# Hybrid block on one core: shift columns partly from transposed weight rows on VectorE, the second V projection and the low-rank projection from rows without shift

## The chip, the cores and the metric

The kernel is one launch on one NeuronCore of a Trainium2 chip. The metric is device time in microseconds; several runs of a kernel are given as their median. A profile is one execution recorded by the hardware profiler.

## The reference, cut to what matters

The program is one layer: a norm with modulation, an input projection, a gated linear attention beside a short convolution, an output projection, a second norm and a feed-forward block. The change touches only the front of it:

```python
mx = silu(c) @ w_mod + b_mod            # c: (2048,), w_mod: (2048, 12288)
mc = silu(c_ctx) @ w_mod + b_mod
sh1, sc1, ... = split(mx, 6)            # shift: columns 0..2047; scale: 2048..4095
hx = rmsnorm(x, norm1_g) * (1 + sc1) + sh1        # x: (512, 2048)
hc = rmsnorm(ctx, norm1_g) * (1 + sc1c) + sh1c    # ctx: (256, 2048)
q, k, v, g, lf, lb, cb, cc, cx = split(hx @ w_in) # for ctx: k, v, lf, lb are needed
```

lf and lb, 16 columns each, are the low-rank projection from which the forget gates come. A projection of `hx` is linear in the shift. So (row without shift) @ w, scaled by the row's norm factor, plus one row sh1 @ w that is the same for all tokens, gives the same values. The kernel uses this, before and after, in different places.

## The kernel before, in words

All operands are fp32. A large product is done as three products of two-part numbers: `split` (L105) writes a high part with ScalarE (L106) and the low rest with VectorE (L107), `split_scaled` and `split_shifted` (L109, L114) do so with a factor or a shift on the way, and `mm3` (L96) issues three matmuls: low times high, high times low, high times high. Every matmul of the front is recorded at L94. Small products are plain fp32 matmuls, which the profile shows as two records each.

Tokens lie along the free dimension: `hx[i]` and `hc[i]`, 16 chunks of 128 channels, each as a high and a low tile, 512 columns for x and 256 for the context. The front has these stages, each a loop over the 16 chunks:

- **K pass** (L254 to L265). `scaled_chunk` multiplies raw rows by the scale alone and accumulates their squares; TensorE makes K from them. After it the norm factors `r6` come, and `rbx`, `rbc`, the same factors along the columns (L284 to L294).
- **First V pass** (L345 to L360). Six accumulators (four token tiles of x, two of the context), 18 matmuls a chunk: V columns 0 to 511, from rows that have neither norm factor nor shift. Beside it, after every fourth chunk, `mod_cols(wsh, ...)` computes the shift of four chunks by small TensorE products: 16 loads of 256 KB from `wsh`, 16 plain matmuls of 512 columns with the 32-column `silu(c)` tile as weights (tile `pm`), a copy `tm`, four small matmuls into `pc` that turn it to columns, four additions of the bias into `shs`. Four chunks later `shift_chunk(i)` rewrites the chunk: GpSimd adds the two parts (L307), VectorE multiplies by the norm factor (L308) and adds the shift (L311), and the sum is split again; for x and for the context. `lf_part` multiplies the low-rank weights with finished x chunks (tile `pl`).
- **Second V pass** (L463 to L478). V columns 512 to 1023 from the rewritten rows, with the last four `shift_chunk` calls. `shares(i)`, 16 calls, loads K and first-V weights again in raw form and makes the products `shs` times weights (tile `pb`): after eight calls the sum is spread to all rows (`pbc`, `pbx`) and added to K or V. The same calls make the context's low-rank products from the old context rows, added up by GpSimd (`hs`, L424).
- Then `weave` (L564) runs the context's states, q, g, the convolution and the attention, and `mod_some` (L380) makes the other four modulation vectors from transposed rows `wm2` with VectorE: a 128x1024 tile times `cbc` (silu(c) on all partitions) summed along the row by one `tensor_tensor_reduce` (L405). Of these loads some are issued by GpSimd, behind a one-element copy that makes them wait (L392).

Order is set by the tile framework: it plans each engine's queue from program order and its own estimate of costs, and may pull an instruction ahead of waiting ones; after that each engine runs its queue strictly in order. So a matmul of `pm` can stand between matmuls of the V pass. SyncE's queue (SP) issues the weight loads in the same way. Raw weight tiles `raw` (128x1024, 512 KB) go through four buffers; `whi` and `wlo`, the split weights, have three each; general tiles `big` have 24. PSUM has three banks of tag "a" and five of tag "g"; a V pass takes three of each.

Of the kernel before, what the change touches and what calls it, by code (L numbers as in the profile page):

```python
# [43 lines left out]

B_ID, B_ONE = range(2)
# [8 lines left out]
def tile_hybrid_block(  # L54
    ctx: ExitStack,
    tc: tile.TileContext,
    xT, cT, xr, ccol, crow, fgrow, cid, cst, sm, cols, gates,
    wsc, wsh, wm2, wk, wv, wl, wq, wg, wc, wo, wu, wd,
# [242 lines left out]
    hraw = {}  # L301

    def shift_chunk(i):

        for n, h, rb, q in ((SEQ, hx[i], rbx, 0), (CTX, hc[i], rbc, 1)):
            t = big() if q == 0 else hcpool.tile([P, n], F32, tag="sq1", name="ht", bufs=2)
            nc.gpsimd.tensor_tensor(t, h[0].bitcast(F32), h[1].bitcast(F32), op=ALU.add)  # L307
            nc.vector.tensor_tensor(t, t, rb, op=ALU.mult)  # L308
            sh = shs[:, i, q : q + 1]
            if q == 0:  # L310
                nc.vector.tensor_scalar(t, t, sh, None, op0=ALU.add)  # L311
                split(h[0], h[1], t)
                hraw[i] = t
            else:
                split_shifted(h[0], h[1], t, sh)
# [6 lines left out]
    def lf_part(pl, g):  # L322

        for j in range(4):
            mm(pl[32 * j : 32 * j + 32, :], wl3[:, 4 * g + j, :], hraw[4 * g + j], g == 0, g == 3)

    def lf_finish(pl, a, n):
# [7 lines left out]
        nc.vector.tensor_copy(lfT[64:96, a : a + n], ps[64:96, :n])  # L335

# [6 lines left out]
    for d in range(2):  # L343
        nc.vector.memset(lfT[64 * d + 32 : 64 * d + 33, :], 1.0)
    accv = banks6()  # L345
    pl = bank("pl")
    for i in range(KD):
# [4 lines left out]
        if i % 4 == 3:  # L352
            pcs = mod_cols(wsh, i - 3, 4)
            for c in range(4):
                nc.vector.tensor_scalar(shs[:, i - 3 + c, 0:2], pcs[:, 2 * c : 2 * c + 2], col(C_BMOD + i - 3 + c),
                                        None, op0=ALU.add)
        if i >= 4:
            shift_chunk(i - 4)
        if i in (8, 12):
            lf_part(pl, i // 4 - 2)  # L360
# [13 lines left out]
    nc.sync.dma_start(cbc, crow.partition_broadcast(P))  # L374
    nc.scalar.activation(cbc, cbc, AF.Silu)
# [40 lines left out]
    def shares(i):  # L416

        if i == 0:
            sh_t["pl"] = bank("pl")
        pl = sh_t["pl"]  # L420
        if i % 2 == 0:
            t = sh_t[i % 4] = hcpool.tile([P, 2, CTX], F32, tag="sq0", name="hs", bufs=2)
            for c in range(2):
                nc.gpsimd.tensor_tensor(t[:, c, :], hc[i + c][0].bitcast(F32), hc[i + c][1].bitcast(F32), op=ALU.add)  # L424
        if i % 4 == 3:
            for c in range(4):
                mm(pl[32 * c : 32 * c + 32, :CTX], wl3[:, i - 3 + c, :], sh_t[c // 2 * 2][:, c % 2, :], i == 3, i == 15)
# [3 lines left out]
        w = load_raw((wk if i < 8 else wv[0])[i % 8]).rearrange("p (k n) -> p k n", k=2)  # L431
# [4 lines left out]
        if i % 8 == 7:  # L436
            t = hcpool.tile([P, SEQ], F32, tag="lfs", name="bs", bufs=1)
            nc.scalar.copy(t, pb)
            pbc = bank("pbc")
            mm(pbc, cstt[:, B_SELC, :], t, True, True)  # L440
            if i < 8:
                for tt in range(NCT):
# [21 lines left out]
    for i in range(KD):  # L464
# [4 lines left out]
        if i < 4:  # L469
            shift_chunk(KD - 4 + i)  # L470
# [876 lines left out]
```

## Time and profile before

| what | us |
|---|---|
| median of 3 runs (2282.64 to 2289.99) | 2288.15 |
| the profiled execution, whole | 2291.32 |
| its span, first to last instruction | 2289.5 |
| first matmul of the first V pass, after the K pass | about 108.2 |
| last small products of the shift (`pc`) | 216.3 |
| first matmul of the next stage (q), after the second V pass | 300.0 |

The profiled execution is 1.8 us longer than its span, and 3.2 us longer than the median. A row of groups reads: line, engine, operation, tile written <- tiles read, shapes, count, then busy time in us and mean ns of one, then idle time before it. A row of the timeline reads: start, duration, engine, line, operation, count merged, and in brackets the idle time before it with what ended it. Matmuls overlap in their pipeline, so the start of the next one is a better measure of what one costs than its duration.

### The profile page before, as it was taken

To read this page: it belongs to the slowest core of one execution; us is meant where nothing else is said; L and a number is where in the kernel's file an instruction comes from. 1 tells how busy PE (TensorE), PEld (TensorE's weight loads), DVE (VectorE), ACT (ScalarE), POOL (GpSimd) and SP (SyncE) were. 2 spreads that over 40 slices of the span, in tenths; PEclk is the share of its full clock that TensorE was granted. 3 is DMA by queue.
4 is the path that set the end of the run, shared out by engine and by line. 5 is a ranking of instruction groups with operands and counts; after the bars stand their busy time and mean duration, and the time that the engine had idled before them with its cause. 6 is when DMAs were issued, how large, how long until landed. Compare 5 with 4: busy or idle time off the path is not lost.

```text
span 2289.5 us, 28001 instructions
## 1 busy us (share of the span) xinstructions
PE 2241.7 (98%) x10258; PEld 1791.7 (78%) x10258; DVE 1658.7 (72%) x2069; ACT 1002.6 (44%) x1354; POOL 251.0 (11%) x396
## 2 busy tenths in 40 slices
PE   8999999999999999999999999999999999999997
PEld 4765666787888887777888888888888878888886
DVE  3566165665768656899788879877987877787885
ACT  3433155333233433665555455445544544433343
POOL 2433100222332000100000000000000000000000
PEclk9999999999999999999999999999999999999999
DMA  9683465566767354624543464345435676756752
GB/s 329 216 279 129 153 221 189 202 220 202 250 228 258 116 198 157 208 69 141 189 156 120 147 210 148 118 159 172 158 131 183 246 291 212 244 193 206 253 174 93
DMA packets 163410, 433.16 MB, mean 189 GB/s; under 512 B 18022, under 2 KB 38790, under 8 KB 163144
## 3 DMA queue, kind: packets, MB, share of 16 engines
q1 hardware_dynamic: 128984, 331.20, 43.3%
q0 software_dynamic: 22416, 78.66, 9.7%
q10 hardware_dynamic: 11872, 21.52, 2.5%
q8 instruction: 81, 1.33, 0.2%
q14 instruction: 57, 0.47, 0.1%
HBM read 380.95 MB, written 50.35 MB: 188 GB/s over the span
## 4 chain that ended last, share of the span: by engine, by line
issue 56%; POOL 2%; PE 1%; DVE 1%; ACT 0%; DMA 0%; POOLq 0%; DVEq 0%; ACTq 0%
POOL opd L1066 2%; PE acc L94 1%; DVE wlo L107 0%; DVE ch L849 0%; DMA out<-g 0%; DVE u L1019 0%; POOL xnd L1022 0%; ACT whi L106 0%; POOL hbig L958 0%; DVE hbig L1020 0%; DVE u L869 0%; POOLq L1066 0%; ACT y L1214 0%; ACT acc L1205 0%; DVE g L1202 0%
## 5 line engine op out<-in xcount | busy, mean ns | idle before, releaser
L106 ACT CAST whi<-ch 128x1024 fp32r<-128x1024 f32 x335 | 352.5, 1053 | 415.4 <-PE acc L94 344.9
L107 DVE TENSOR_TENSOR wlo<-ch,whi 128x1024 fp32r<-128x1024 f32 x335 | 408.2, 1223 | 126.9 <-ACT whi L106 126.0
L106 ACT CAST whi<-raw 128x1024 fp32r<-128x1024 f32 x258 | 270.7, 1050 | 453.6 <-PE acc L94 282.0
L107 DVE TENSOR_TENSOR wlo<-raw,whi 128x1024 fp32r<-128x1024 f32 x258 | 316.6, 1227 | 198.3 <-ACT whi L106 197.7
L94 PE MATMUL acc<-hhl,whi 128*128 128x512 f32 x640 | 200.0, 393 | 0.0
L94 PEld LDWEIGHTS acc<-hhl,whi 128*128 128x128 f32 x640 | 120.8, 189 | 27.6 <-issue 2.5
L1066 POOL DMA_DIRECT2D opd<-ol x80 | 43.3, 541 | 885.8 <-DVE ol L107 885.7
L94 PE MATMUL acc<-hhi,wlo 128*128 128x512 f32 x320 | 134.1, 421 | 5.4 <-DVE wlo L107 4.6
L405 DVE CUSTOM_DVE_ANT_0 wm<-wm,cbc 128x1024 f32<-128x1024 f32 x66 | 80.6, 1224 | 80.9 <-DMA wm<-wm 80.2
L94 PE MATMUL acc<-wlo,a0h 128*128 128x512 f32 x324 | 128.8, 397 | 4.0 <-DVE wlo L107 4.0
L94 PE MATMUL acc<-whi,a6l 128*128 128x512 f32 (+1 forms) x330 | 127.9, 389 | 2.4 <-ACT acc L1205 2.1
L94 PE MATMUL acc<-wlo,a6h 128*128 128x512 f32 (+1 forms) x330 | 128.1, 388 | 1.3 <-DVE wlo L107 1.3
L94 PE MATMUL acc<-whi,a6h 128*128 128x512 f32 (+1 forms) x330 | 127.8, 387 | 0.0
L94 PE MATMUL acc<-whi,a0h 128*128 128x512 f32 x324 | 127.5, 393 | 0.0
L94 PE MATMUL acc<-hlo,whi 128*128 128x512 f32 x320 | 126.9, 397 | 0.2 <-DVE hlo L112 0.2
L94 PE MATMUL acc<-hhl,wlo 128*128 128x512 f32 x320 | 127.0, 397 | 0.0
L94 PE MATMUL acc<-whi,a0l 128*128 128x512 f32 x324 | 126.9, 393 | 0.0
L94 PE MATMUL acc<-whi,a5h 128*128 128x512 f32 x324 | 126.3, 390 | 0.0
L94 PE MATMUL acc<-hhi,whi 128*128 128x512 f32 x320 | 126.2, 394 | 0.0
L94 PE MATMUL acc<-whi,a5l 128*128 128x512 f32 x324 | 126.2, 389 | 0.0
L94 PE MATMUL acc<-wlo,a5h 128*128 128x512 f32 x324 | 126.1, 389 | 0.0
L405 DVE CUSTOM_DVE_ANT_0 raw<-raw,cbc 128x1024 f32<-128x1024 f32 x62 | 75.4, 1223 | 51.4 <-DMA raw<-wm 51.1
(334 smaller groups left out, 4991.8 us busy)
## 6 DMA issues: line engine op xcount, KB each, us to landing
raw<-wu SPq DMA_DIRECT2D x92, 512.0 KB, 4.4
ch<-wu SPq DMA_DIRECT2D x88, 512.0 KB, 3.8
wm<-wm POOLq DMA_DIRECT2D x66, 512.0 KB, 5.3
raw<-wd SPq DMA_DIRECT2D x50, 512.0 KB, 5.3
raw<-wc SPq DMA_DIRECT2D x48, 512.0 KB, 4.7
opd<-oh ACTq DMA_DIRECT2D x80, 256.0 KB, 3.2
opd<-ol POOLq DMA_DIRECT2D x80, 256.0 KB, 3.7
ch<-wd SPq DMA_DIRECT2D x38, 512.0 KB, 4.4
```

What stands on the lines that cost most here:

```text
L94: nc.tensor.matmul(o, l, r, start=start, stop=stop, skip_group_check=True)
L106: nc.scalar.copy(hi, src)
L107: (eng or nc.vector).tensor_tensor(lo, src, hi, op=ALU.subtract)
L405: nc.vector.tensor_tensor_reduce(out=w, in0=w, in1=cbc[:, hf * 1024 : hf * 1024 + 1024], scale=1.0, scalar=0.0, op0=ALU.mult, op1=ALU.add, ...
L1066: nc.gpsimd.dma_start(opd[j][i, 1].rearrange("p k t -> p (k t)"), lo.bitcast(F32))
```

## The change

**Shift.** The first four chunks of the shift still come from `mod_cols`, now after chunk 1. The other twelve come from `wst`, the same columns of `w_mod` laid out transposed: for each chunk a 128x2048 block, loaded in two halves of 512 KB by GpSimd's queue into the four `raw` buffers. Each half is multiplied and summed by VectorE three times: two products of 512 columns with silu(c_ctx) (four `big` tiles `ccbc`), one of 1024 columns with silu(c) (`cbc`, loaded earlier than before). After each eight halves two small sums and two bias additions write four chunks of `shs`. There are 24 halves: 20 in the first V pass, four in the first two chunks of the second.

**Second V pass from rows without shift.** It uses the same rows as the first. Its evictions scale by the norm factor (`from_banks`), and its share of the shift comes from a third group of `shares` with raw weights, eight more loads and 16 more small products, spread and added as the others are. `shift_chunk(i)` rewrites x chunk i only when both V passes have read it; the context's rows are not rewritten at all.

**Low rank from rows without shift.** In the first V pass `lf_part` is called after chunks 4, 7, 10 and 13: GpSimd adds up four x chunks and four context chunks, TensorE makes 4 + 4 products. `lf_finish` multiplies by the norm factor. The shift's share of it comes in `lf_shift`, after chunk 3 of the second V pass, by 16 products of two columns.

```diff
@@ tile_hybrid_block @@
+NPE = 4
     def shift_chunk(i):
-        for n, h, rb, q in ((SEQ, hx[i], rbx, 0), (CTX, hc[i], rbc, 1)):
-            t = big() if q == 0 else hcpool.tile([P, n], F32, tag="sq1", name="ht", bufs=2)
-            nc.gpsimd.tensor_tensor(t, h[0].bitcast(F32), h[1].bitcast(F32), op=ALU.add)
-            nc.vector.tensor_tensor(t, t, rb, op=ALU.mult)
...
+        h, t = hx[i], big()
+        nc.gpsimd.tensor_tensor(t, h[0].bitcast(F32), h[1].bitcast(F32), op=ALU.add)
+        nc.vector.tensor_tensor(t, t, rbx, op=ALU.mult)
+        split_shifted(h[0], h[1], t, shs[:, i, 0:1])
+    def lf_part(plx, plc, g):
+        tx, tcx = [big() for _ in range(4)], []
+        for c in range(4):
+            i = 4 * g + c
+            if c % 2 == 0:
+                t2 = hcpool.tile([P, 2, CTX], F32, tag="sq0", name="hs", bufs=2)
+            tcx.append(t2[:, c % 2, :])
+            for t, h in ((tx[c], hx[i]), (tcx[c], hc[i])):
+                nc.gpsimd.tensor_tensor(t, h[0].bitcast(F32), h[1].bitcast(F32), op=ALU.add)
+        for pl, t, n in ((plx, tx, SEQ), (plc, tcx, CTX)):
+            for c in range(4):
+                mm(pl[32 * c : 32 * c + 32, :n], wl3[:, 4 * g + c, :], t[c], g == 0, g == 3)
     def lf_finish(pl, a, n, rb):
-        nc.scalar.copy(t[:, :n], pl[:, :n])
+        nc.vector.tensor_tensor(t[:, :n], pl[:, :n], rb, op=ALU.mult)
+    def lf_shift():
+        plb, t, b = bank("plb"), modv[:, 16:18], modv[:, 20:22]
+        for k in range(KD):
+            j = 32 * (k % 4)
+            mm(plb[j : j + 32, 0:2], wl3[:, k, :], shs[:, k, 0:2], k < 4, k >= 12)
...
+    nc.sync.dma_start(cbc, crow.partition_broadcast(P))
+    nc.scalar.activation(cbc, cbc, AF.Silu)
+    ccbc = [big() for _ in range(4)]
+    for q in range(4):
+        nc.sync.dma_start(ccbc[q], ccrow[q * 512 : q * 512 + 512].partition_broadcast(P))
+        nc.scalar.activation(ccbc[q], ccbc[q], AF.Silu)
+    def shift_rows(halves, w0):
+        for _ in range(halves):
+            n, hf = divmod(done[0], 2)
+            done[0] += 1
+            w = wpool.tile([P, 1024], F32, tag="raw", name="raw", bufs=4)
+            nc.gpsimd.tensor_copy(w[:, 0:1], w0[0][:, 0, 0:1].bitcast(F32))
+            nc.gpsimd.dma_start(w, wst[n, :, hf * 1024 : hf * 1024 + 1024])
+            for q in (2 * hf, 2 * hf + 1):
+                nc.vector.tensor_tensor_reduce(
+                    out=waste, in0=w[:, q % 2 * 512 : q % 2 * 512 + 512], in1=ccbc[q], scale=1.0, scalar=0.0,
+                    op0=ALU.mult, op1=ALU.add, accum_out=accc[:, n, q : q + 1])
+            nc.vector.tensor_tensor_reduce(
+                out=w, in0=w, in1=cbc[:, hf * 1024 : hf * 1024 + 1024], scale=1.0, scalar=0.0,
+                op0=ALU.mult, op1=ALU.add, accum_out=accx[:, n, hf : hf + 1])
+            if done[0] % 8 == 0:
...
     for i in range(KD):          # first V pass
-        if i % 4 == 3:
-            pcs = mod_cols(wsh, i - 3, 4)
...
-        if i >= 4:
-            shift_chunk(i - 4)
-        if i in (8, 12):
-            lf_part(pl, i // 4 - 2)
+        if i == 1:
+            pcs = mod_cols(wsh, 0, NPE)
...
+        shift_rows(2 if i % 4 == 1 else 1, wvp)
+        if i in (4, 7, 10, 13):
+            if i == 4:
+                plx, plc = bank("plx"), bank("plc")
+            lf_part(plx, plc, i // 3 - 1)
+    lf_finish(plx, 0, SEQ, rbx)
+    lf_finish(plc, SEQ, CTX, rbc)
     def shares(i):
...
-        w = load_raw((wk if i < 8 else wv[0])[i % 8]).rearrange("p (k n) -> p k n", k=2)
+        w = load_raw((wk, wv[0], wv[1])[i // 8][i % 8]).rearrange("p (k n) -> p k n", k=2)
...
+        if i % 8 == 7 and i < 16:
+            shared(i // 8)
     for i in range(KD):          # second V pass
-        if i < 4:
-            shift_chunk(KD - 4 + i)
-        if i == 1:
-            lf_part(pl, 2)
-        elif i == 5:
-            lf_part(pl, 3)
-            lf_finish(pl, 0, SEQ)
-        if i > 5:
-            for k in ((2 * i - 12, 2 * i - 11) if i < 12 else (i,)):
-                shares(k)
...
+        if i < 2:
+            shift_rows(2, wvp)
+        else:
+            for k in (0, 1) if i == 2 else (i - 1,):
+                shift_chunk(k)
+        if i == 3:
+            lf_shift()
+        if i > 3:
+            shares(2 * i - 8)
+            shares(2 * i - 7)
+    from_banks(1)
+    shift_chunk(KD - 1)
+    shared(2)
```

`shared(g)` is the old end of `shares` (spread and add) as a function, with g = 2 for the second half of V. On the host, `wsh` is cut to the first 512 columns and `wst` is the transpose of the other 1536.

More of the change, by code (lines that the diff above doesn't have):

```diff
@@ L320, in stat, with lf_finish @@
         return sl(hc[i], ALL, slice((tt - NX) * P, (tt - NX) * P + P))
[L322 to L327, printed above, removed]
+    def lf_part(plx, plc, g):
[10 more added lines that the diff above has]
+                mm(pl[32 * c : 32 * c + 32, :n], wl3[:, 4 * g + c, :], t[c], g == 0, g == 3)
+    def lf_finish(pl, a, n, rb):
         t = hcpool.tile([P, SEQ], F32, tag="lfs", name="lfs", bufs=1)
-        nc.scalar.copy(t[:, :n], pl[:, :n])
+        nc.vector.tensor_tensor(t[:, :n], pl[:, :n], rb, op=ALU.mult)
         ps = bank("ps")
@@ L416, in shares @@
     def shares(i):
[L418 to L427, printed above, removed]
         if i % 8 == 0:
@@ new lines, in shares, with shared @@
+        if i % 8 == 7 and i < 16:
+            shared(i // 8)
+    def shared(g):
+        t = hcpool.tile([P, SEQ], F32, tag="lfs", name="bs", bufs=1)
+        nc.scalar.copy(t, sh_t["pb"])
+        pbc = bank("pbc")
+        mm(pbc, cstt[:, B_SELC, :], t, True, True)
+        if g == 0:
+            for tt in range(NCT):
+                nc.vector.scalar_tensor_tensor(kc[tt], kc[tt], r6[:, NX + tt : NX + tt + 1], pbc,
+                                               op0=ALU.mult, op1=ALU.add)
+            pbk = bank("pbk")
+            for h in range(HEADS):
+                mm(pbk[:, 2 * h : 2 * h + 2], tok(t, h), selt, h == 0, True)
+            bk = hcpool.tile([P, 8], F32, name="bk")
+            nc.vector.tensor_copy(bk, pbk[:, :8])
+            for h in range(HEADS):
+                nc.vector.tensor_scalar(kT[h], kT[h], bk[:, 2 * h : 2 * h + 1], None, op0=ALU.add)
+            return
+        for tt in range(NCT):
+            nc.vector.tensor_tensor(vc[tt][g - 1], vc[tt][g - 1], pbc, op=ALU.add)
+        pbx = bank("pbx")
+        mm(pbx, cstt[:, B_SELX, :], t, True, True)
+        for hh in range(2):
+            for t2 in range(2):
+                for u in range(2):
+                    v = vx[2 * g - 2 + hh][t2][:, u, :]
+                    nc.vector.tensor_tensor(v, v, pbx[:, hh * DV : hh * DV + DV], op=ALU.add)
@@ new lines, in from_banks @@
+    def from_banks(g):
+        for tt in range(NX):
+            for hh in range(2):
+                if tt % 2 == 0:
+                    vx[2 * g + hh][tt // 2] = xpool.tile([P, 2, DV], F32, tag="t", name="vx")
+                nc.scalar.activation(vx[2 * g + hh][tt // 2][:, tt % 2, :], accv[tt][:, hh * DV : hh * DV + DV],
+                                     AF.Copy, scale=r6[:, tt : tt + 1])
+        for tt in range(NCT):
+            vc[tt][g] = big()
+            nc.vector.tensor_scalar(vc[tt][g], accv[NX + tt], r6[:, NX + tt : NX + tt + 1], None, op0=ALU.mult)
```

79 lines of the change are left out of this document (27 added, 52 removed).

## The prediction

> **What bounds the kernel now.** I read the page first for the busy engine, then the windows of the two V passes, then TensorE's timeline inside them, and then VectorE and GpSimd, to which the change gives work.
>
> ```profile
> span 2289.5 us, 28001 instructions
> PE 2241.7 (98%) x10258; PEld 1791.7 (78%) x10258; DVE 1658.7 (72%) x2069; ACT 1002.6 (44%) x1354; POOL 251.0 (11%) x396
> ```
>
> TensorE is busy nearly all the time; VectorE has room as an average. The change concerns two stages only, so their own rows count (columns: window, then the busy time of PE, PEld, DVE, ACT and POOL with instruction counts, granted clock, share of the DMA engines, GB/s).
>
> ```profile
> 108.20:216.20 108.00, 106.04 (x500) 66.73 (x499) 69.52 (x105) 34.84 (x55) 39.48 (x32) 1.00 0.66 222
> 216.20:300.00 83.80, 83.73 (x411) 56.46 (x409) 25.12 (x42) 15.58 (x27) 12.11 (x16) 1.00 0.41 139
> ```
>
> The first is the first V pass with the shift products, the second the second V pass with the shares. TensorE fills both, at full clock. So TensorE time removed here shortens the kernel, until another engine or a transfer ends last. VectorE has 38 us free in the first window and 59 in the second: the change puts most of its new VectorE work in the first.
>
> **What it removes.** One chunk of the V pass and one of the four sets of shift products stand so in TensorE's timeline:
>
> ```profile
> 150.62 0.39 PE L94 MATMUL acc<-whi,hhl 128*128 128x512 f32 x1
> 150.84 0.39 PE L94 MATMUL acc<-whi,chl 128*128 128x512 f32 x1
> 151.07 0.39 PE L94 MATMUL acc<-wlo,chl 128*128 128x512 f32 x1
> ...
> 152.30 2.78 PE L94 MATMUL pm<-big,silsh 128*32 128x512 f32 x24
> 155.01 0.50 PE L94 MATMUL acc<-whi,hlo 128*128 128x512 f32 x1
> ...
> 155.81 0.40 PE L94 MATMUL acc<-whi,hlo 128*128 128x512 f32 x1
> 156.77 1.72 PE L94 MATMUL pm<-big,silsh 128*32 128x512 f32 x4 [0.57 <-DMA big<-wsh]
> 158.43 0.50 PE L94 MATMUL acc<-wlo,hhi 128*128 128x512 f32 x1
> ...
> 159.32 1.04 PE L94 MATMUL pm<-big,silsh 128*32 128x512 f32 x2
> 160.30 0.50 PE L94 MATMUL acc<-wlo,hhi 128*128 128x512 f32 x1
> ...
> 161.19 1.05 PE L94 MATMUL pm<-big,silsh 128*32 128x512 f32 x2
> 162.17 0.50 PE L94 MATMUL acc<-wlo,hhi 128*128 128x512 f32 x1
> ...
> 163.20 0.95 PE L94 MATMUL pc<-smt,tm 128*128 128x2 f32 x8
> 164.01 0.70 PE L94 MATMUL acc<-whi,chl 128*128 128x512 f32 x2
> ```
>
> V matmuls start 0.227 us apart (150.62, 150.84, 151.07). The set costs, from the start of its piece to the next V matmul: 2.71 us, then 2.39 (155.81 plus 0.23 for that matmul, to 158.43, with a wait for a load in it), 0.98, 0.98, and 0.81 for the turn into columns: 7.87 us. Twelve products that follow each other directly take 0.23 us each, a single one 0.98. Three such sets go: 23.6 us. By the group's busy time it is a little less:
>
> ```profile
> L94 PE MATMUL pm<-big,silsh 128*32 128x512 f32 x128 | 25.9, 598 | 2.0 <-DMA big<-wsh 1.8
> L94 PEld LDWEIGHTS pm<-big,silsh 128*32 128x32 f32 x128 | 5.0, 109 | 15.4 <-issue 8.6 <-DMA big<-wsh 6.8
> ```
>
> Three quarters of 25.9 are 19.4, and three times 0.81 make 21.9. I take 23.
>
> **What it adds on TensorE.** The nearest rows are those of the shares:
>
> ```profile
> 247.08 1.06 PE L94 MATMUL pb<-raw,silsh 128*32 128x512 f32 x8
> ...
> 282.70 1.05 PE L94 MATMUL pb<-raw,silsh 128*32 128x512 f32 x4
> ...
> 298.58 0.64 PE L94 MATMUL pl<-hs,big 128*32 128x256 f32 x8
> ...
> 301.06 1.02 PE L94 MATMUL pbc<-bs,cstt 128*128 128x512 f32 x2
> 301.92 1.02 PE L94 MATMUL pbx<-bs,cstt 128*128 128x512 f32 x2
> ```
>
> Four products side by side (eight records, each of the four in its own 32 columns) take 1.06 us, and two take 1.05. Today 32 products stand in six blocks of four and four blocks of two, 10.6 us; then 48 stand in twelve blocks of four, 12.7: plus 2.1. Spreading the third group costs one `pbc` and one `pbx`, each 0.86 by starts: 1.7. `lf_shift` has 16 products of two columns, 32 records that load 32 columns of weights: at 0.109 us a load 3.5 us, less if loads overlap; with its two small sums 3.9. That row doesn't exist before; from below, four at a time as in `pb`, it would be near 1 us. I take 3.9. The context's low-rank products leave the second pass, where some lie beside `pb`, and stand alone in the first, 0.64 us for four: I count 0.7 for the lost overlap. The x part moves at no change. Added: 2.1 + 1.7 + 3.9 + 0.7 = 8.4 us.
>
> TensorE alone: 23 less 8.4, so 14.6 us less. The first pass itself loses 23 and takes over low-rank products (four x blocks of about 1 us, two of them new here, 2.1; the context's, 2.5; two sums, 1.7), so it lasts some 91 us.
>
> **What it adds on VectorE and GpSimd.** The product with a sum exists already for the later modulation vectors, and a 512-wide operation on two SBUF tiles too:
>
> ```profile
> 308.82 1.22 DVE L405 CUSTOM_DVE_ANT_0 raw<-raw,cbc 128x1024 f32<-128x1024 f32 x1
> 309.97 0.08 DVE L405 DVE_READ_ACCUMULATOR2_ANT modacc<- 128x1 f32 x1
> 309.97 1.22 DVE L405 CUSTOM_DVE_ANT_0 raw<-raw,cbc 128x1024 f32<-128x1024 f32 x1
> ...
> 118.81 1.89 DVE L371 TENSOR_TENSOR big<-big 128x512 f32<-128x512 f32 x3
> ```
>
> A product of 1024 takes 1.15 us from start to start, and the reading of its sum lies inside the next. A 512-wide operation takes 0.63. A half thus costs 1.15 + 2 x 0.63 = 2.41 us: 48 us for the 20 halves of the first pass, 10 for the four of the second. The weight splits of the pass, eight of 1.15, are 9; the rest (norm chain, scaling K, evictions, `lf_finish`) I put at 14, which stands for what remains of this window's 69.5 when its rewriting is gone. VectorE: 71 us of 91. It fits, if VectorE is left alone. It is not:
>
> ```profile
> 130.08 1.28 POOL L307 TENSOR_TENSOR big<-hhi,hlo 128x512 f32<-128x512 f32 x1 [22.40 <-PE pm L94]
> 130.09 2.35 DVE L107 TENSOR_TENSOR wlo<-raw,whi 128x1024 fp32r<-128x1024 f32 x1 [5.14 <-ACT whi L106]
> ...
> 146.44 0.74 POOL L424 TENSOR_TENSOR hs<-chl 128x256 f32<-128x256 f32 x1
> ...
> 208.43 1.26 POOL L307 TENSOR_TENSOR big<-hhi,hlo 128x512 f32<-128x512 f32 x1
> ...
> L308 DVE TENSOR_TENSOR big<-big 128x512 f32<-128x512 f32 x16 | 18.4, 1182 | 3.5 <-POOL big L307 3.5
> ```
>
> A split of 1.22 us began 0.01 us after a GpSimd addition of 1.28 and took 2.35: it stood still for nearly the whole addition. L308, 0.63 alone, averaged 1.18 beside GpSimd. The new low-rank path puts 16 additions of 512 (1.26) and 16 of 256 (0.74) into the first pass: 32 us of GpSimd, and its new load issues wait in the same queue for free buffers, so a late VectorE holds up the additions too. In the L308 rows 16 operations lost 0.55 us each to additions of 1.26, 44%. At that rate VectorE loses 14 us of the 32 and stands at 85 of 91. That fits with little room, and the splits for the next weights queue behind the products in VectorE's order, as TensorE's weights do behind the splits; the products themselves start only when the activated rows have come. The bounds of what reaches TensorE are 0 and 71 + 32 - 91 = 12. I take 6, the middle, because the row nearest to it (L308) also has about half.
>
> In the second pass VectorE has 10 for halves, 9 for splits, 16 x 2 x 0.63 = 20 for rewriting and some 11 for shares and evictions, 50 us, and GpSimd 16 x 1.26 = 20: 70 of about 85. That hides them; uncovered, `lf_shift`, which needs the last half, would hold TensorE's queue for the lateness of the products. I leave that inside the 6.
>
> **Transfers.** The shift's bytes are the same, 16.8 MB, of which 2 MB now move to the second pass. The activated rows for the context add 1 MB of spread copies.
>
> ```profile
> wm<-wm POOLq DMA_DIRECT2D x66, 512.0 KB, 5.3
> ...
> raw<-wv SPq DMA_DIRECT2D x24, 512.0 KB, 4.6
> ...
> SPq L122 <- DVE wlo L107: 60.4, 10, 19.7
> ```
>
> A landing on GpSimd's queue takes 5.3 us, a weight load 4.6. Today SyncE waits 60 us in front of weight loads for a buffer whose split is done: weights lie ready far ahead. After the change 20 halves and eight weights share four buffers. A half holds one for 5.3 + 2.41 = 7.7 us at least, a weight for 4.6, a cast of about 1 and 1.15, 6.8: 208 us over four buffers, 52 of 91. That covers it, with 39 us to spare for waiting.
>
> **Sum.** 14.6 less 6, so 8.6 us less: the profiled execution 2291.3 becomes 2282.7. It lay 3.2 above the median of the runs, so the median 2288.15 becomes about 2280. The measurement can tell 0.3%, 6.9 us, from no change.
>
> **The rivals.** First, products beside GpSimd cost TensorE nothing, since only the splits matter and three of each are kept ahead: then the full 14.6, 2273.5. For it speaks that SyncE's wait shows weights far ahead today, against it that the buffers are now shared.
>
> Second, every GpSimd addition stands in front of VectorE in full: 12 us reach TensorE, with 2 more for a late start of the products, and the gain is gone: 14.6 less 14, 2287.5. The row at 130.09 speaks for it, the mean of L308 against it. [...]
>
> Third, on the other side: the four raw buffers decide. If a tile holds its buffer for more than 13 us (91 x 4 / 28) the ring paces the pass, and the weight load waits in it like the rest. VectorE's queue of two halves and a split, 6 us, with collisions some 8 to 9, brings 7.4 on the mean to 16: 28 x 16 / 4 = 112 us, 21 over 91, and 6.5 us slower than before, about 2295. Against it: it needs a full queue for the whole pass. From 14.6 us of idle TensorE on it is slower.
>
> **Chances.** Forecast, 2275 to 2286: 0.42, of it 0.25 below 2281.3 and 0.17 above. First rival 0.25, second 0.16, third 0.17. Faster by over 0.3%: 0.25 + 0.25 = 0.50. Within 0.3%: 0.17 + 0.16 = 0.33. Slower: 0.17. The range goes from 2270 (first rival, with 23.6 removed and `lf_shift` at 1 us) to 2297 (the third with a hold somewhat above 16); some 0.15 lies outside.
>
> **What would show it.** In the profile after: `pm` with 32 records in the first pass, and no wait of it for loads after about 140 us; 24 products of 1024 near 1.22 us where GpSimd rests and above 2 where it adds; between the first V matmul and the first matmul of q 183 us instead of 191.8. Idle TensorE in front of V matmuls, released by `wlo` on VectorE, is the 6 us: near 0 confirms the first rival, 14 the second. Released by the cast or by a load `raw<-wv`, with SyncE waiting for products at L122, it is the third. A long wait before `plb` would show `lf_shift` as the place. The forecast is wrong if the stages after q change their length, if a 512-wide product costs more than 0.7 us undisturbed, or if the idle time of both passes exceeds 12 us.

## The result and the profile after

The changed kernel takes 2315.01 us in the median of 4 runs (2313.09 to 2319.37), the kernel before beside it 2289.07: a ratio of 1.0124, 95% interval 1.0109 to 1.0139. It is slower by 1.2%, 25.9 us, where 8.6 us less was forecast. The profiled execution took 2315.5 us. From its page:

```profile
span 2313.7 us, 27992 instructions
PE 2239.9 (97%) x10210; PEld 1791.4 (77%) x10210; DVE 1709.2 (74%) x2184; ACT 998.7 (43%) x1338; POOL 290.4 (13%) x444
```

TensorE has 48 instructions less and is busy 1.8 us less, while the span is 24.2 us longer. So it stood still longer, and the windows show where (columns as in the prediction):

```profile
100.00:150.00 50.00, 45.93 (x170) 27.24 (x168) 28.51 (x56) 14.60 (x21) 23.49 (x33) 0.93 0.52 185
150.00:200.00 50.00, 40.86 (x175) 27.94 (x177) 31.49 (x66) 4.68 (x5) 28.91 (x37) 0.93 0.43 147
200.00:250.00 50.00, 38.88 (x177) 27.91 (x177) 41.98 (x73) 9.73 (x16) 25.70 (x32) 0.86 0.49 156
250.00:300.00 50.00, 46.35 (x243) 31.54 (x242) 33.11 (x48) 10.34 (x15) 12.12 (x8) 0.93 0.48 162
```

TensorE is idle 28 us in these 200, and its granted clock, 1.00 in both windows of before, is 0.86 to 0.93. VectorE is not full in any of them either: 42 of 50 us at the most, with the time in it that it stood blocked. What TensorE waited for between 105 and 330 us (total, times, longest):

```profile
PE ps L96 <- DVE lfs L333: 11.0, 1, 11.0
PE acc L96 <- DVE wlo L109: 7.8, 5, 3.1
PE acc L96 <- ACT whi L108: 4.5, 3, 2.8
...
PE plb L96 <- DVE silsh L399: 1.6, 1, 1.6
```

The longest wait, for the scaled low rank (`lfs`), begins on VectorE. First VectorE's timeline around it, then GpSimd's:

```profile
228.84 6.22 DVE L390 CUSTOM_DVE_ANT_0 raw<-raw,cbc 128x1024 f32<-128x1024 f32 x1
...
235.60 1.40 DVE L427 TENSOR_SCALAR big<-acc,rs_r 128x512 f32<-128x512 f32 x2
236.93 0.41 DVE L333 TENSOR_TENSOR lfs<-plc,big 128x256 f32<-128x256 f32 x1
```
```profile
228.51 0.53 POOL L385 DMA_DIRECT2D raw<-wst  x1 [0.41 <-POOL raw L384]
229.06 1.27 POOL L307 TENSOR_TENSOR big<-hhi,hlo 128x512 f32<-128x512 f32 x1
230.28 1.26 POOL L307 TENSOR_TENSOR big<-hhl 128x512 f32<-128x512 f32 x1
231.50 1.26 POOL L307 TENSOR_TENSOR big<-hhi,hlo 128x512 f32<-128x512 f32 x1
232.72 1.25 POOL L307 TENSOR_TENSOR big<-hhl 128x512 f32<-128x512 f32 x1
```

One product of 1.22 us lasted 6.22: by the records it began 0.22 us before a row of four GpSimd additions and ended 1.09 us after the last of them (232.72 plus 1.25), which is about the rest of its own work. Behind it in VectorE's queue stood `lfs`, and TensorE behind that.

At the front of the stage the first weights are late. Rows of ScalarE and of SyncE's queue:

```profile
110.01 1.92 ACT L367 ACTIVATE cbc<-cbc 128x2048 f32<-128x2048 f32 x1
...
112.42 1.28 ACT L149 ACT_TABLE_LOAD   x1
...
113.82 1.03 ACT L108 CAST whi<-raw 128x1024 fp32r<-128x1024 f32 x1
```
```profile
87.60 29.38 SPq L124 DMA_DIRECT2D raw<-wv  x2
...
119.87 17.96 SPq L202 DMA_DIRECT2D big<-wsh  x16
137.93 0.37 SPq L124 DMA_DIRECT2D raw<-wv  x1
```

The Silu of the conditioning row and a table load stand in front of the first cast; the marker copies of the first halves wait for that cast (GpSimd's L384 begins at 114.91); and no weight load is issued between 117 and 137.93, as the shift's 16 loads stand in SyncE's queue.

After waits TensorE ran at half speed (granted clock 0.50 in five stretches between 100 and 340 us; from 238 to 242 us it is the longest wait that stands ahead). Starts of V matmuls after a wait of 2.78 us are 0.43 us apart, and 0.23 from 198 us on; after one of 3.15 us they were 0.23 apart at once:

```profile
168.58 0.50 PE L96 MATMUL acc<-wlo,hhi 128*128 128x512 f32 x1 [3.15 <-DVE wlo L109]
168.91 0.39 PE L96 MATMUL acc<-whi,hhi 128*128 128x512 f32 x1
169.15 0.40 PE L96 MATMUL acc<-whi,hlo 128*128 128x512 f32 x1
...
194.81 0.79 PE L96 MATMUL acc<-wlo,hhi 128*128 128x512 f32 x1 [2.78 <-DVE wlo L109]
195.40 0.63 PE L96 MATMUL acc<-whi,hhi 128*128 128x512 f32 x1
195.82 0.63 PE L96 MATMUL acc<-wlo,hhi 128*128 128x512 f32 x1
...
198.44 0.39 PE L96 MATMUL acc<-whi,chl 128*128 128x512 f32 x1
198.67 0.39 PE L96 MATMUL acc<-wlo,chl 128*128 128x512 f32 x1
```

The trace shows a raster in this. Between 100 and 340 us the granted clock changes at 116.06, 122.89, 180.91, 184.33, 194.57, 197.98, 228.70, 242.35, 259.42 and 266.25 us, always a multiple of 3.41 us apart. The last window of 3.41 us ahead of the fall at 194.57 and the one after it:

```profile
191.16:194.57 3.41, 0.86 (x3) 0.37 (x3) 3.38 (x7) 0.00 (x0) 2.27 (x4) 1.00 0.28 103
194.57:197.98 3.41, 3.17 (x8) 2.50 (x9) 3.33 (x9) 0.00 (x0) 0.03 (x1) 0.50 0.82 240
```

The wait of 2.78 us fell nearly whole into the first, and TensorE was busy there for 0.86 us. The wait of 3.15 us lay across two windows (from 163.85 and 167.26), busy for 1.58 and 2.10 us, and the clock stayed full. So the length of a wait alone does not tell whether the clock falls: the longer of these two kept it.

An account of TensorE from the first `pss` (109.5 before, 110.7 after) to the first gate product `pzs` (305.0, 333.3), worked out from its timeline: from each start to the next, less the wait named; what a V matmul takes above 0.2275 us is counted as slow clock where it is 0.12 to 0.35 us. For later use it has three experiments too.

| us | before | after | e7 | e11 | e18 |
|---|---|---|---|---|---|
| V matmuls | 141.3 | 141.1 | 139.3 | 138.3 | 139.1 |
| shift products and `pc` | 28.1 | 13.4 | 11.8 | 9.7 | 9.8 |
| shares `pb`; `pbc`, `pbx` | 10.6 | 16.1 | 16.1 | 16.2 | 16.1 |
| low rank with `plb` | 7.9 | 7.7 | 12.2 | 12.1 | 9.4 |
| small ones (`pss`, `pr`, `ps`, `pbk`) | 4.8 | 7.0 | 6.9 | 5.1 | 5.0 |
| named waits | 1.8 | 28.1 | 8.0 | 3.2 | 4.7 |
| slow clock | 1.0 | 9.2 | 2.5 | 0.0 | 0.1 |
| sum | 195.5 | 222.6 | 196.8 | 184.5 | 184.2 |

After less before: own work 7.4 less, waits 26.3 more, slow clock 8.2 more, together 27.1 more. The split between the first row and the slow clock hangs on where that line is drawn, by a microsecond or so; their sum doesn't. In the kernel before, ten matmuls of q stand ahead of that gate product and are counted among the V matmuls, 2.3 us at 0.2275 each, and in none of the others: like for like the stage's own work fell by 5.1. That stage began 1.2 us later, and the stages behind it took some 4 less, 2.3 of it these ten matmuls.

### The profile page after: what moved, and what is told of

Same layout as the page of the kernel before. It is cut to its first block, busy times and chain, and to the rows that moved or that the text cites. A ratio compares the mean times of both kernels' runs of the same rounds, so it can differ in the third digit from the quotient of the medians.

```text
span 2313.7 us, 27992 instructions
## 1 busy us (share of the span) xinstructions
PE 2239.9 (97%) x10210; PEld 1791.4 (77%) x10210; DVE 1709.2 (74%) x2184; ACT 998.7 (43%) x1338; POOL 290.4 (13%) x444
## 4 chain that ended last, share of the span: by engine, by line
issue 30%; PE 25%; DVE 3%; POOL 1%; DMA 0%; ACT 0%; POOLq 0%; DVEq 0%; ACTq 0%
PE acc L96 24%; DVE wlo L109 1%; POOL opd L1122 1%; PE pt L1108 1%; DVE ch L905 0%; PE pt L1026 0%; DVE u L925 0%; DMA raw<-wu 0%; DVE ch L886 0%; DVE hbig L1076 0%; DMA out<-g 0%; DVE u L1075 0%; DVE a2l L109 0%; DVE a6l L109 0%; DVE s L832 0%
## 5 line engine op out<-in xcount | busy, mean ns | idle before, releaser
L109 DVE TENSOR_TENSOR wlo<-raw,whi 128x1024 fp32r<-128x1024 f32 x258 | 315.6, 1224 | 141.1 <-ACT whi L108 140.5
L96 PEld LDWEIGHTS acc<-hhl,whi 128*128 128x128 f32 x640 | 120.6, 189 | 26.3 <-issue 1.2
L96 PE MATMUL acc<-whi,a1l 128*128 128x512 f32 x268 | 105.5, 394 | 2.2 <-DVE a1l L109 2.2
```

The costliest lines, as they stand in the source:

```text
L96: nc.tensor.matmul(o, l, r, start=start, stop=stop, skip_group_check=True)
L109: (eng or nc.vector).tensor_tensor(lo, src, hi, op=ALU.subtract)
```

## The experiments

Three theories were open. *Capacity*: VectorE, with its own work and what GpSimd's additions take, is too full. *Buffers*: rows and weights share four `raw` buffers. *Queue*: GpSimd's one queue, run in order, holds the row loads, which wait for casts and buffers, and the additions, for which TensorE and VectorE wait; what is late in it is late for all. Every edit also lets the framework plan the queues anew, so a difference is that of the edit with the plan that it gets. All ratios are to the kernel before, which ran beside each group of runs (2287.8 to 2289.2).

**Without rows.** The loads and products of twelve chunks are left out, so the shift of these chunks is missing.

```diff
-        for _ in range(halves):
+        for _ in range(0):
```

> The changed kernel without its shift rows: no loads of the transposed rows and none of their 72 products, so twelve of the sixteen shift chunks are left out (they stay zero); all else is as changed. It measures the other part alone: second V projection and low rank from rows without shift, and one set of shift products instead of four. Queue theory (the halves reserve raw buffers, SyncE's queue stands still and all behind it comes late) and collision theory (GpSimd's additions stop VectorE's products) both expect that TensorE's account holds here: 2289 less 14.6, 2270 to 2280 us. If it is above 2290, the rearranged low rank and second pass are slow by themselves and the rows are not the cause.

Measured: 2279.32, ratio 0.9964 (0.9951 to 0.9977), 35.7 us below the changed kernel. So the whole loss, and more, hangs on the rows and what they meet.

**Halves after chunk 3.**

```diff
-        shift_rows(2 if i % 4 == 1 else 1, wvp)
+        if i > 2:
+            shift_rows(2 if i % 2 else 1, wvp)
```

> The halves begin after chunk 3 instead of chunk 0, two after each odd chunk, 20 in the first pass as before the edit. The first weights, the activated rows and the loads of the four PE-made shift chunks then come ahead of them. Queue theory: SyncE's wait of 20 us at the end of the K pass is gone, the shift products stand in one piece again (7 us less), VectorE's idle 12 and 9 us in the first pass shrink: 2295 to 2303 us. Collision theory: products and additions are packed closer, so no gain: 2313 to 2320.

Measured: 2328.99, 1.0176 (1.0151 to 1.0200), slower still and above both expected ranges: waits for `wlo` grew to 17.1 us and for `whi` to 8.4. A crowded start isn't the cause by itself; the same rows in less time cost more.

**Halves loaded by SyncE.**

```diff
-            w = wpool.tile([P, 1024], F32, tag="raw", name="raw", bufs=4)
-            nc.gpsimd.tensor_copy(w[:, 0:1], w0[0][:, 0, 0:1].bitcast(F32))
-            nc.gpsimd.dma_start(w, wst[n, :, hf * 1024 : hf * 1024 + 1024])
+            w = load_raw(wst[n, :, hf * 1024 : hf * 1024 + 1024])
```

> The halves are loaded by SyncE's queue without the one-element copy, instead of GpSimd's. The buffers stay shared. Queue theory: the three empty reserved buffers fill at once at the end of the K pass, and halves no longer wait behind GpSimd's additions (VectorE's 9.3 us idle for a row load at 164.8 goes), but the second weight still has to wait for a buffer: 2298 to 2310 us. Collision theory: the additions still stop the products, 2312 to 2318.

Measured: 2303.7, 1.0069 (1.0049 to 1.0090): 11.3 us of the loss come back.

**No additions on GpSimd in these stages.** `lf_part` multiplies the two parts of a chunk one after the other, and `shift_chunk` adds on VectorE.

```diff
-        nc.gpsimd.tensor_tensor(t, h[0].bitcast(F32), h[1].bitcast(F32), op=ALU.add)
+        nc.vector.tensor_tensor(t, h[0].bitcast(F32), h[1].bitcast(F32), op=ALU.add)
...
-                mm(pl[32 * c : 32 * c + 32, :n], wl3[:, 4 * g + c, :], t[c], g == 0, g == 3)
+                for part in range(2):
+                    mm(pl[32 * c : 32 * c + 32, :n], wl3[:, 4 * g + c, :], hs[4 * g + c][part].bitcast(F32),
+                       g == 0 and part == 0, g == 3 and part == 1)
```

> No additions on GpSimd in the two V passes: the low-rank products take the high and the low part as two products each (32 more small ones, about 7 us of TensorE side by side), and the addition in the rewriting of a chunk is on VectorE (16 more of 0.63 us). Collision theory: no product above 1.3 us, the wait of 11 us for the low-rank eviction and most of those for weight splits go: 2290 to 2300. Queue theory: SyncE's 20 us wait, the scattered shift products and VectorE's idle time up to 153 us remain, only the halves behind the additions come sooner: 2305 to 2317.

Measured: 2307.63, 1.0084 (1.0062 to 1.0106): 7.4 us back, although the low rank now costs TensorE some 4 us more.

**No context products.** The 48 products of 512 columns are left out, so the context's shift of the twelve chunks is missing; VectorE's work on a half falls from 2.4 to 1.15 us.

```diff
+    nc.vector.memset(accc, 0.0)
...
-            for q in (2 * hf, 2 * hf + 1):
-                nc.vector.tensor_tensor_reduce(
-                    out=waste, in0=w[:, q % 2 * 512 : q % 2 * 512 + 512], in1=ccbc[q], scale=1.0, scalar=0.0,
-                    op0=ALU.mult, op1=ALU.add, accum_out=accc[:, n, q : q + 1])
```

> The changed kernel without the 48 products of 512 columns for the context's shift: that part is left out (the sums stay zero), and VectorE's work for a half falls from 2.4 to 1.15 us; loads, buffers, queues and additions stay. Capacity theory (VectorE's work, slowed by GpSimd, sets the pace): most of the 36 us that the rows cost goes, 2285 to 2297 us. Buffer theory (four raw buffers and the queues behind them set it): little goes, 2305 to 2315.

Measured: 2314.43, 1.0107 (1.0087 to 1.0127), no change, as *buffers* or *queue* would have it. So *capacity* is out: half of VectorE's new work could go and nothing was gained. Its windows, and VectorE and GpSimd around its longest wait:

```profile
150.00:200.00 50.00, 46.55 (x224) 32.93 (x225) 23.91 (x32) 5.73 (x6) 30.07 (x42) 1.00 0.50 172
200.00:250.00 50.00, 31.43 (x137) 22.23 (x136) 38.11 (x45) 9.97 (x17) 23.33 (x27) 0.80 0.46 155
```
```profile
218.61 10.73 DVE L387 CUSTOM_DVE_ANT_0 raw<-raw,cbc 128x1024 f32<-128x1024 f32 x1 [3.19 <-POOL big L307]
```
```profile
217.26 1.27 POOL L307 TENSOR_TENSOR big<-hhi,hlo 128x512 f32<-128x512 f32 x1
218.48 1.26 POOL L307 TENSOR_TENSOR big<-hhl 128x512 f32<-128x512 f32 x1
...
227.01 1.25 POOL L307 TENSOR_TENSOR big<-hhi,hlo 128x512 f32<-128x512 f32 x1
```

VectorE had 26 us free in the one window and 12 in the other, yet one product stood behind a row of additions for 10.73 us, and TensorE waited 17.3 us for `lfs`.

**Own buffers.** The rows come as quarters of 256 KB in `big` tiles; the `raw` buffers hold weights alone.

```diff
-            w = wpool.tile([P, 1024], F32, tag="raw", name="raw", bufs=4)
...
             for q in (2 * hf, 2 * hf + 1):
+                w = big()
+                nc.gpsimd.tensor_copy(w[:, 0:1], w0[0][:, 0, 0:1].bitcast(F32))
+                nc.gpsimd.dma_start(w, wst[n, :, q * 512 : q * 512 + 512])
```

> The rows come in quarters of 256 KB into general tiles instead of halves into the four raw buffers, still on GpSimd's queue behind the copy; the 1024-wide product becomes two of 512 (0.1 us more a half). The weights have the raw buffers to themselves again. Buffer theory: SyncE's waits for products at L124 go and weights lie ahead, 2290 to 2302 us. Capacity theory: splits still queue behind products on VectorE, 2308 to 2318.

Measured: 2340.14, 1.0222 (1.0205 to 1.0239), slower by another 25 and above both expected ranges: `plb` waits 18.0 us for the last sums and `plx` 12.1 for GpSimd's additions, which now stand behind twice the marker copies and loads. SyncE no longer waits for products there (71.2 us in the changed kernel, none here), so the `raw` buffers alone are not the cause. The run changes two things, though, and can't say what own buffers would be worth with GpSimd's queue as it was; a fuller queue of GpSimd makes it worse.

**Both jobs off GpSimd's queue** (the edits of e3 and e4 together).

> Two edits together: halves loaded by SyncE, and no additions on GpSimd in the two V passes. If both edits heal different waits their gains add up: 2315 less 11 less 7, 2294 to 2299 us. If both heal the same wait (halves behind additions in GpSimd's queue), it stays at 2301 to 2306.

Measured: 2291.56, 1.0016 (1.0001 to 1.0031): 23.4 us back, 4.7 more than 11.3 and 7.4 make, and below both expected ranges. VectorE's products (48 of 512 columns and 24 of 1024) are at their undisturbed length, 687 and 1225 ns on the mean; in the changed kernel they averaged 810 and 1562:

```profile
L379 DVE CUSTOM_DVE_ANT_0 big<-raw,big 128x512 f32<-128x512 f32 x48 | 33.0, 687 | 1.6 <-ACT big L365 0.9
L382 DVE CUSTOM_DVE_ANT_0 raw<-raw,cbc 128x1024 f32<-128x1024 f32 x24 | 29.4, 1225 | 0.7
```
```profile
L387 DVE CUSTOM_DVE_ANT_0 big<-raw,big 128x512 f32<-128x512 f32 x48 | 38.9, 810 | 23.1 <-DMA raw<-wst 17.1 <-POOL hs L325 3.5 <-ACT big L371 1.7
L390 DVE CUSTOM_DVE_ANT_0 raw<-raw,cbc 128x1024 f32<-128x1024 f32 x24 | 37.5, 1562 | 0.6
```

**And later sums**: e7 with `lf_finish` called after chunk 3 and `lf_shift` after chunk 4 of the second pass.

```diff
-    lf_finish(plx, 0, SEQ, rbx)
-    lf_finish(plc, SEQ, CTX, rbc)
...
+            lf_finish(plx, 0, SEQ, rbx)
+            lf_finish(plc, SEQ, CTX, rbc)
+        if i == 4:
             lf_shift()
```

> As the one before, and the low-rank sums are taken after chunk 3 of the second V pass instead of between the passes, the shift's share after chunk 4: TensorE's queue no longer has the sums in front of the second pass. If the wait for the low-rank eviction is a stall of its own, 4 to 8 us less than the run before; if it only moves to the next thing that needs VectorE, no more than 2 us.

Measured: 2292.79, 1.0021 (1.0008 to 1.0034). No gain: the wait for `lfs` falls from 3.0 to 1.3 us, another of 1.1 comes.

**Chunk additions alone on VectorE**: the first hunk of e4 alone, on the changed kernel (e9) and on e3 (e10).

> The changed kernel with one line altered: the sixteen additions of shift_chunk (hi plus lo of each rewritten chunk, 1.26 us each on GpSimd) go to VectorE; the row loads stay in GpSimd's queue, and so do the additions of the low rank. If what costs is that additions stand back to back in front of one VectorE product (the product of 6.22 us at 228.84, and the wait of 10.99 us behind it), the wait for the scaled low rank is gone and with it the slow clock behind it: 2297 to 2303 us. If what costs is the one queue that holds loads and additions between 115 and 217 us of the span, the waits for the split weights stay and only a part of the 10.99 us comes back: 2305 to 2312.

> As e3_by_sync (halves of rows issued by SyncE, no marker copy), and the additions of shift_chunk on VectorE as well; the additions of the low rank stay on GpSimd, so that TensorE's small products are not doubled (about 6 us less TensorE work than in e7_sync_no_gpsimd). If it is the chunk additions that keep e3_by_sync at 2303.7, this comes to 2286 to 2293, at or below e7_sync_no_gpsimd. If it is the low rank's additions (40 of them among the products of the rows), it stays at 2300 to 2304.

Measured: e9 2309.79, 1.0086 (1.0073 to 1.0098); the wait for `lfs` fell from 11.0 to 6.4 us, those for `wlo` (7.7) and `whi` (4.7) stayed, as the queue theory has it. e10 2293.88, 1.0018 (1.0007 to 1.0030): with the loads on SyncE the chunk additions were what kept e3 up, and the low rank's sums on GpSimd (32 of them, not 40) seemed to cost little beyond one wait of 6.9 us.

**The first weights ahead of the conditioning rows**: on e7 (e11), and with the one set of shift products behind chunk 3 (e12).

```diff
-    nc.sync.dma_start(cbc, crow.partition_broadcast(P))
-    nc.scalar.activation(cbc, cbc, AF.Silu)
     ccbc = [big() for _ in range(4)]
-    for q in range(4):
...
             wvp = load_w(wv[0, i // 2], 2)
+        if i == 0:
+            nc.sync.dma_start(cbc, crow.partition_broadcast(P))
+            nc.scalar.activation(cbc, cbc, AF.Silu)
+            for q in range(4):
+                nc.sync.dma_start(ccbc[q], ccrow[q * 512 : q * 512 + 512].partition_broadcast(P))
+                nc.scalar.activation(ccbc[q], ccbc[q], AF.Silu)
```
```diff
-        if i == 1:
+        if i == 3:
             pcs = mod_cols(wsh, 0, NPE)
```

> As e7_sync_no_gpsimd, with the first weights of the V projection loaded and cast ahead of the two conditioning rows (their five DMAs and five Silus come behind the load of the first weights). If the wait of 2.8 us for the first cast and the slow clock behind it are the rows' price at the front, 2286 to 2289 us. If the halves, which need these rows, then start later and end later, the wait comes back at the end of the stage: 2291 to 2295.

> As e11_weights_first, with the one set of shift products that is left on TensorE placed behind chunk 3 of the projection, where the first of the four sets stood before the change, not behind chunk 1. If the set is cut into twos there because its loads come one by one (12.4 us where a set took 7.9), it comes in one piece behind chunk 3 and saves 3 to 4 us: 2282 to 2286 us, level with the kernel before or just below it. If its 16 loads stand in front of the rows and weights in SyncE's queue wherever they are, no gain or a loss: 2287 to 2294.

Measured: e11 2277.94, 0.9948 (0.9935 to 0.9962), the fastest of all with e18: 13.6 us below e7, where at most 5.6 was expected, and 11.3 below the kernel before. e12 2279.17, 0.9958 (0.9945 to 0.9970), no better; the set costs the same 8.6 us there, and its loads a wait of 2.5. In e11 the cast is at 107.81 (113.82 after), ahead of the Silu, and these waits are left:

```profile
107.81 1.05 ACT L108 CAST whi<-raw 128x1024 fp32r<-128x1024 f32 x1
...
113.47 1.92 ACT L394 ACTIVATE cbc<-cbc 128x2048 f32<-128x2048 f32 x1
```
```profile
PE ps L96 <- DVE lfs L327: 1.4, 1, 1.4
PE pbc L96 <- ACT bs L481: 0.8, 1, 0.8
...
PE acc L96 <- ACT whi L108: 0.2, 1, 0.2
```

The account compares e7 with e11: of 12.3 us less, 4.8 are waits, 2.5 slow clock, and 5 matmuls that take less time from start to start, shift products (2.1) and small ones (1.8) above all.

**The same move elsewhere.** Was the front the root? It was moved alone in the changed kernel (e13), in e3 (e14), e10 (e15) and e4 (e16).

> The changed kernel with one thing moved: the first weights of the V projection are loaded and cast ahead of the five conditioning-row DMAs and their Silus. Row loads and additions stay on GpSimd. If the late first cast is the root (marker copy, raw buffers and halves all late behind it), most of the loss comes back: 2285 to 2293 us. If it is a price of its own beside those of GpSimd's queue (13.6 us, e7_sync_no_gpsimd less e11_weights_first), 2299 to 2304.

> As e3_by_sync (halves issued by SyncE) with the first weights ahead of the conditioning rows; all additions stay on GpSimd. If prices add: 2303.7 less 13.6, 2288 to 2292 us. If the additions cost only because the halves ran late beside them, 2274 to 2281.

> As e10_sync_chunk_sums (halves by SyncE, shift_chunk's additions on VectorE, the low rank's sums on GpSimd) with the first weights ahead of the conditioning rows. TensorE does some 5 us less than in e11_weights_first, whose low-rank products are doubled. If only the front was wrong there, 2271 to 2276 us; if the wait for the low rank's sums (6.9 us in e10_sync_chunk_sums) stays, 2277 to 2282.

> As e4_no_gpsimd_adds (no additions of the low rank or of rewritten chunks on GpSimd; row loads with marker copies in its queue) with the first weights ahead of the conditioning rows. If prices add: 2307.6 less 13.6, 2292 to 2296 us. If the loads on GpSimd's queue cost only through the late first cast, as e11_weights_first: 2275 to 2282.

Measured, with the gain of the move over the kernel without it:

| kernel | us | ratio to before (95%) | the move gave |
|---|---|---|---|
| e13, on the changed kernel | 2312.24 | 1.0103 (1.0084 to 1.0121) | 2.8 |
| e14, on e3 | 2301.01 | 1.0062 (1.0049 to 1.0074) | 2.7 |
| e15, on e10 | 2296.52 | 1.0043 (1.0030 to 1.0056) | -2.6 |
| e16, on e4 | 2297.26 | 1.0035 (1.0019 to 1.0050) | 10.4 |
| e11, on e7 | 2277.94 | 0.9948 (0.9935 to 0.9962) | 13.6 |

Neither of the two readings holds for e13, e14 and e15: the front is neither the root nor a price that adds. The gain in e13 is not clear of the noise; its interval and that of the changed kernel (1.0109 to 1.0139) overlap. Where the low rank's sums stay on GpSimd the move gives 3 us or nothing, without them 10 to 14. In e15 GpSimd and TensorE show why:

```profile
134.53 1.27 POOL L325 TENSOR_TENSOR big<-hhi,hlo 128x512 f32<-128x512 f32 x1 [24.94 <-PE pm L96]
```
```profile
159.18 2.69 PE L96 MATMUL plc<-hs,big 128*32 128x256 f32 x7 [9.04 <-POOL hs L325]
```

The sums wait 24.9 us for tiles that the shift's loads hold, and TensorE, whose queue has the low rank's products early, stands 9.0 us for them. A sooner start of the stage is only a longer wait there.

**Without the marker copy** (e16 less that line), and **the low rank's sums on VectorE** (e15 with `nc.vector` for them, so that TensorE's products are not doubled).

```diff
-            nc.gpsimd.tensor_copy(w[:, 0:1], w0[0][:, 0, 0:1].bitcast(F32))
```
```diff
-                nc.gpsimd.tensor_tensor(t, h[0].bitcast(F32), h[1].bitcast(F32), op=ALU.add)
+                nc.vector.tensor_tensor(t, h[0].bitcast(F32), h[1].bitcast(F32), op=ALU.add)
```

> As e16_no_gpsimd_first without the marker copy: a row load on GpSimd's queue goes out as soon as its buffer is free, and does not wait for the cast of the weights before it. If the loop of cast, marker, row load and buffer is the price, the time comes down to that of e11_weights_first, 2276 to 2284 us. If it is the four buffers that rows and weights share, whoever issues, 2292 to 2300.

> As e11_weights_first, but with the low rank from single sums (32 additions, now on VectorE, and not 64 products on TensorE): TensorE has some 4.5 us less to do in the stage (plx and plc 11.7 us there, 7.2 in the changed kernel), VectorE some 18 us more beside the 48 products. If VectorE is not the bound, 2272 to 2275 us; if it is, waits for wlo or for the sums take its place: 2279 to 2290.

Measured: e17 2286.2, 0.9988 (0.9976 to 1.0000), 11.1 of the 19.3 us between e16 and e11. So the marker copy is the larger part of what the loads cost on GpSimd there, where no additions stand in its queue; from where the other 8.3 come is open. In e16 one sees the loop: a weight load that comes late behind rows keeps a cast waiting, and the evictions of the pass (`vx`) stand behind that cast on ScalarE; TensorE waits 6.4 us for them, and its V matmuls after that start 0.43 us apart, up to 228.60 us.

```profile
218.45 1.04 ACT L108 CAST whi<-raw 128x1024 fp32r<-128x1024 f32 x1 [12.86 <-DMA raw<-wv]
219.40 3.03 ACT L418 ACTIVATE vx<-acc,rs_r 128x256 f32<-128x256 f32 x8
```

e18: 2278.11, 0.9952 (0.9938 to 0.9966), level with e11. The 32 sums on VectorE fill it more than anything tried here:

```profile
150.00:200.00 50.00, 50.00 (x233) 37.29 (x233) 49.20 (x117) 7.04 (x9) 0.00 (x0) 1.00 0.64 206
200.00:250.00 50.00, 48.00 (x253) 33.17 (x253) 48.39 (x93) 14.27 (x24) 1.05 (x2) 1.00 0.59 197
```

VectorE is busy 49.2 of 50 us, with splits and products in one queue, and TensorE is busy all 50 at full clock. Of the 2.7 us that the low rank saves there, 1.5 are given back in waits (4.7 us for 3.2; those for `wlo` and `whi` are 1.6 and 1.5) and 0.8 in V matmuls, so this is about where VectorE begins to tell.

## Why the prediction was wrong, point by point

- **The step that failed** is the size of what reaches TensorE: "The bounds of what reaches TensorE are 0 and 71 + 32 - 91 = 12. I take 6". Waits rose by 26.3 us and the slow clock by 8.2. The step asked whether VectorE's work and its collisions fit into the pass, and let only what did not fit reach TensorE. They do fit: the products lost (810 - 687) x 48 + (1562 - 1225) x 24 ns, 14.0 us, and VectorE was never full. That the prediction's sum has 14 us too is chance. Its 14 were for the first pass; there products and weight splits lost 4.6 us by the trace, and the other 9.8 of the 14.0 fell in the second, 5.0 of them in one product. What failed is the upper bound of 12: a delay reached TensorE though the work fitted.

  The prediction had seen the road ("its new load issues wait in the same queue for free buffers, so a late VectorE holds up the additions too") and gave it no price in the sum. Queues that run in order carry a delay from engine to engine: cast to marker copy, marker copy to row load and addition, addition to product, product to split or `lfs`, that to TensorE. e5 (half the products, no gain), e7 (queue free, 23.4 us back) and e18 (VectorE at 49.2 of 50, no loss against e11) show it together. The sign that it named for the 6 us, waits for `wlo`, came to 7.8; the longest wait, 11.0 for `lfs`, is in none of its signs.
- **The rate of 44%**, the mean of L308, hid that collisions were not spread evenly here. One product lost 5.0 us to a row of four additions, one in e5 9.5 to a row of eight, where a single addition cost a split 1.13. The second rival had the single block right, with the row at 130.09 behind it: there a split that began 0.01 us after an addition took 2.35 us, here a product that began 0.22 us before a row of four stood until all four had ended. But not every addition blocked, as the products lost 14.0 us beside some 52 us of additions (32 and 20 in the prediction's sums). The rival's price, 12 us on a capacity that was never used up, was not what came.
- **The third rival**, slower, 2295, had the signs that came: SyncE's queue waited 71.2 us at its weight loads (L124) for products of L390, and casts 59.1 us for loads `raw<-wv`. But its mechanism, four buffers as the pace of the pass, fell with e11 and e18: rows and weights share the four buffers there too, and the loss is gone. The waits came from the order of the queues, with the marker copy as a large part of it in e16 (11.1 us, e17); the prediction's sum has no term for that copy.
- **The start of the stage** was not costed: the words "2 more for a late start of the products" stood for it in one rival. The conditioning rows, with one Silu and a table load ahead of the first cast and four more loads ahead of the later weights, cost 2.8 us of wait at the place, and 13.6 once the rest is mended (e7 against e11).
- **The shift sets**: 23 us removed were forecast, 14.7 came from products and `pc` (28.1 to 13.4), with 1.8 of waits for loads before. The set that was read, 7.87 us with a wait of 0.57 in it, was a dear one: four took 28.1 in the account, 7.0 each. The set that is left came in pairs between V matmuls, as its 16 loads were issued over 18 us, and took 12.4 us. In e11 it took 8.7, and 18.4 were removed.
- **What TensorE gets more** was about right: 7.5 us for 8.4, though by terms that were off both ways, so the near total is partly luck. `pb` took 3.2 for 2.1, `pbc` and `pbx` 2.3 for 1.7 (in the trace before, a `pbx` took 0.46 by starts, 301.92 to 302.38, not 0.86). `lf_shift` was too dear: its 32 records of `plb` took 0.5 us less the wait, for 3.5; the waits at it were 1.6 for `plb` and 1.6 for its small sums. The low rank with `plb` took 0.2 less, where 0.7 and the 3.5 were added. Small sums and norm products took 2.2 more; 1.4 of it are the norm products (`pr`), most of which ran at half clock after the first wait, a term that the sum did not have.
- **Where the forecast was right** in kind: TensorE's own work is what limits, once waits are gone. e11 and e18 stand 11.0 and 11.3 us below before in the account, 8.7 and 9.0 without the ten matmuls of q, and 11.3 and 10.7 in the medians (2277.94 against 2289.23, 2278.11 against 2288.79; the executions of the account differ by 13.4 and 8.1), where the sum of TensorE said 14.6. The products are 1.22 us undisturbed, and the stages behind kept their length but for some 2 us beside these ten matmuls.
- By its own test, wrong "if the idle time of both passes exceeds 12 us", it is wrong: 28.1.

What stays open is how the 25.9 us split between GpSimd's blocking, its queue and the new plan of the queues: gains of single edits don't add, and each edit changes the plan. Twelve of the eighteen runs came out outside both ranges expected of them, three of these by about 1 us (e10, e16, e18), so the account explains the waits that the traces show but does not yet forecast a time. That the two jobs in that queue together with the late first cast make up the loss is shown by e11 and e18: they move these three things to other engines or another place, keep all rows and their products, and the loss is gone.

## What to carry to other kernels

Work that fits by sum can still cost more than its sum: follow each new instruction down the queue in which it stands, and ask who waits behind it and what that one holds. Keep loads that wait for a buffer, and any copy that is there to make them wait, out of a queue whose arithmetic another engine needs (e7: 23.4 us back). Mend waits together: one alone may give 3 us (e13) that gives 14 after the next (e11).

## What the runs showed of the hardware

- Two VectorE products of 1024 columns (`raw` by `cbc`) that started beside a row of GpSimd additions ended only after the row (6.22 us beside four in the changed kernel, 10.73 beside eight in e5, 1.22 undisturbed). By the records the first began 0.22 us before its row, the second 0.13 us after the first of its eight. In e15 both sides were longer instead, over a stretch of more than 10 us: products of 0.69 us took 1.6 to 1.7, additions of 1.27 took 1.7 to 2.2. First VectorE's rows, then GpSimd's:

```profile
147.86 1.74 DVE L380 CUSTOM_DVE_ANT_0 big<-raw,big 128x512 f32<-128x512 f32 x1
...
149.64 1.63 DVE L380 CUSTOM_DVE_ANT_0 big<-raw,big 128x512 f32<-128x512 f32 x1
```
```profile
146.81 2.24 POOL L325 TENSOR_TENSOR big<-hhi,hlo 128x512 f32<-128x512 f32 x1
149.01 1.71 POOL L325 TENSOR_TENSOR big<-hhl 128x512 f32<-128x512 f32 x1
```

- In the changed kernel waits of 2.78, 2.82 and 10.99 us were followed by 3 to 4 us of V matmuls 0.43 us apart, one of 3.15 us was not. Its granted clock changed only on a raster of 3.41 us. The five windows of it ahead of a fall to 0.50 had TensorE busy for 0.86 to 1.61 us; after one with 1.58 us, all of it V matmuls, the clock stayed at 1.00, so the busy time alone doesn't tell either. The slow stretches cost 9.2 us in the changed kernel, a third as much as the waits.
- The plain fp32 products with two columns out (`plb`) cost next to nothing here: 32 records in 0.5 us by starts, less a wait of 1.55.
